# A list scheduler that keeps each PSUM bank to one engine at a time

## The chip, the cores and the metric

The kernel runs as one program on one core of a Trainium2 chip. The metric is the device time of one execution in microseconds (us). A core has five engines with in-order queues of their own: TensorE (PE), which multiplies matrices and writes its results into PSUM; VectorE (DVE) and ScalarE (ACT), which read PSUM and compute element by element; GpSimd (POOL), which here works on SBUF alone; and SyncE (SP), which issues the DMAs. PSUM has eight banks of 512 float32 numbers in each of 128 partitions. Engines wait for each other through semaphores.

## The reference

Two layers of a hybrid mixer work on 128 prompt tokens and 512 sample tokens, 640 in all, of width 1024, in float32. A layer normalises and modulates the input, projects it, sends the parts through three branches (latent attention, differential attention, a chunked mLSTM), gates each branch and projects back:

```python
h = rmsnorm(x, W['g_norm'][l]) * (1 + scale) + shift
proj = h @ W['W_in'][l]
...
o1 = attention(q_b[..., :DIFF_D], keys_b[..., :DIFF_D], vals_b, DIFF_SCALE)
o2 = attention(q_b[..., DIFF_D:], keys_b[..., DIFF_D:], vals_b, DIFF_SCALE)
o_b = rmsnorm(o1 - lam.astype(o1.dtype) * o2, W['diff_norm'][l]) * (1.0 - lam_init)
...
sw = jnp.einsum('bhtd,bhsd->bhts', qc, kc) * w_intra
...
y = jnp.concatenate([o_a.reshape(B, T, GROUP_W) * jax.nn.silu(z_a),
                     o_b.reshape(B, T, GROUP_W) * jax.nn.silu(z_b),
                     o_c.reshape(B, T, GROUP_W) * jax.nn.silu(z_c)], axis=-1) @ W['W_out'][l]
x_new = x + gate * y
```

## The kernel before

**Recording and planning.** The kernel's body does not issue instructions. Every call on an engine is recorded by `Plan.add`, and at the end `Plan.issue` links the operations by their data (`link`), plays them through a list scheduler (`simulate`) and issues them in the order of the start times that the scheduler gave. So every instruction of the profile has one line, L488, and places in the program have to be told by tile shapes and times. In `simulate` each engine takes, whenever it is free, the ready operation with the lowest number (program order) for which `may` finds its tiles' places vacant. An operation is ready when all operations that it depends on by data have ended by the costs of `cost` and the delays of `delay`.

**Data and banks.** `link` finds dependencies by the elements that operations touch. Only for PE does it keep a rule on whole banks (a matmul follows the last matmul in its bank). The program built from the order, on the other hand, gets its semaphore waits when it is issued, in the order of issue: two instructions of different engines on the same PSUM bank are put one behind the other there, also where they touch different elements or only read. Which of two such instructions goes first is therefore decided by the global order that the plan gives, not only by the order on each engine.

**Where engines share a bank.** Three helpers matter.

- `k_stack` (L1180): in the preparation of each of the four differential heads of a layer (`diff_prep`), PE transposes the head's keys into a two-bank tile `pkd`. ACT makes four rounded copies of 64 partitions by 640 columns (two maps, each copied to two halves of a stack) and four of 64 by 128; DVE subtracts each from the PSUM values for the low part. In the profile these are ACT `CAST slotsr<-banks` and DVE `TENSOR_TENSOR slotsr<-banks,slotsr`. The scores of that head use them some microseconds later.
- `attend` (L1193): probabilities are transposed into PSUM (PE `banks<-fix,slots 128x128`), copied by ACT to SBUF (`COPY slots<-banks`) and multiplied with the values on PE. For the prompt tokens (t = 4) this is one 128x128 transposition, one small ACT copy, one matmul.
- `pst` (L1102) in each mLSTM head: five 128x128 score matmuls of PE into one two-bank tile (`banks<-slots 128x128`), each then read by a DVE multiplication (`fix<-fix,banks 128x256`).

The weights come in 512 KB pieces through three raw buffers. ACT casts each piece to a high part (`CAST fixr<-fix`), and DVE or POOL computes the low part, which frees the raw buffer and lets SP issue the next load.

Of the kernel before, what the change touches and what calls it, by code (L numbers as in the profile page):

```python
# [121 lines left out]
class Plan:  # L122
# [87 lines left out]
    def free(ap):  # L210
# [2 lines left out]
            n *= s  # L213
        return n

    def cost(self, o):


        m, e, k = o["m"], o["eng"], o["k"]
        if m == "dma_start":  # L220
            out = o["outs"][0]
            return 430, 0, 4 * self.free(out) * int(out.shape[0]), False
        if e == "PE":
            if m == "transpose":
                return 109, 273, 0, False
            n = self.free(k["rhs"])
            if "float32r" in str(k["rhs"].dtype):
                return max(111, 0.4535 * n + 3), 175 + 0.4535 * n, 0, False
            return 2 * max(111, 0.845 * n), 280 + max(0, 0.845 * n * 2 - 110), 0, False
        if not o["outs"]:  # L230
            return 60, 60, 0, False
        n = max(self.free(x) for x in o["outs"] + o["ins"])
        ptr = any(self.is_ap(x) and self.free(x) == 1 and n > 2 for x in list(o["a"][1:]) + [k.get("scale"), k.get("bias")])
        psum = any("PSUM" in str(x.space) for x in o["ins"])
        if e == "ACT":
            t = 155 + 0.85 * n + (100 if ptr else 0) + (193 if "accum_out" in k else 0)
            if any("Ln" in str(x) for x in o["a"]):
                return t + 2500, t + 1300, 0, False
            return t - 95, t, 0, False
        two = m in ("tensor_tensor", "tensor_tensor_scan", "scalar_tensor_tensor")  # L240
        if e == "DVE":
            t = 145 + 1.06 * n
            if m == "tensor_copy" and not psum or m == "memset":
                t = 145 + 0.53 * n
            elif m == "tensor_tensor_scan":
                t = 145 + 2.08 * n
            elif ptr:
                t += 62
            return t - 80, t, 0, not psum and (two or m == "tensor_copy" or m == "tensor_scalar" and n > 1)
        if "pow" in str(k.get("op")):  # L250
            t = 400 + 155 * n
        elif m == "memset":
            t = 145 + 0.75 * n
        else:
            t = 165 + 2.2 * n
        return t - 40, t, 0, two
# [6 lines left out]
    def link(self):  # L263
        last, readers = {}, {}
        for i, o in enumerate(self.ops):
            pre, tiles = set(), set()
            for x in o["ins"]:
                n = x.tensor.name
                if n in self.tags:
                    tiles.add(n)  # L270
                if n.startswith("in_") or n.startswith("out_"):
                    continue
                for key, m in self.touch(x).items():
                    for w, wm in last.get(key, ()):
                        if wm & m:
                            pre.add(w)
                    readers.setdefault(key, []).append((i, m))
            for x in o["outs"]:
                n = x.tensor.name
                if n in self.tags:  # L280
                    tiles.add(n)
                if n.startswith("in_") or n.startswith("out_"):
                    continue
                for key, m in self.touch(x).items():
                    kept = []
                    for r, rm in readers.get(key, ()):
                        if rm & m:
                            if r != i:
                                pre.add(r)
                            rm &= ~m  # L290
                        if rm:
                            kept.append((r, rm))
                    if key in readers:
                        readers[key] = kept
                    kept = []
                    for w, wm in last.get(key, ()):
                        if wm & m:
                            if w != i:
                                pre.add(w)
                            wm &= ~m  # L300
                        if wm:
                            kept.append((w, wm))
                    kept.append((i, m))
                    last[key] = kept
            if o["eng"] == "PE":

                x = o["outs"][0]
                key = (x.tensor.name, int(x.offset) % int(x.tensor.shape[-1]) // 512)
                pre.update(last.get(key, ()))
                last[key] = [i]  # L310
            pre.discard(i)
            o["pre"], o["tiles"] = pre, tiles
            o["occ"], o["lat"], o["bytes"], o["port"] = self.cost(o)

    def simulate(self, prio, strict=None, place=None):
# [3 lines left out]
        n = len(ops)  # L319
        pre = [set(o["pre"]) for o in ops]  # L320
        if strict is not None:
            tail = {}
            for i in strict:
                e = ops[i]["eng"]
# [9 lines left out]
        vacant, bank = {i: -1.0 - i for i in range(43)}, place or {}  # L334
# [11 lines left out]
        have, queue = set(), {b: list(l) for b, l in self.tenants.items()} if place else {}  # L346
# [3 lines left out]
        ev, start, dma, port, cold = [], [0.0] * n, 0.0, 0.0, 0.0  # L350
# [3 lines left out]
        t = end = 0.0  # L354
        done = 0

        def may(o):
            for x in o["tiles"]:
                if x not in have:
                    tag = self.tags[x][0]  # L360
                    if place:
                        if not all(b in vacant and queue[b][0] == x for b in place[x]):
                            return False

                    elif live[tag] + rank[x] - nxt[tag] - sum(y < rank[x] for y in early[tag]) >= self.CAPS[tag]:
                        return False
                    elif not any(all(b in vacant for b in c) for c in self.PLACES[tag]):
                        return False
            return True
        while done < n:  # L370
            moved = True
            while moved:
                moved = False
                for e in ready:
# [4 lines left out]
                    while ready[e]:  # L379
                        it = heappop(ready[e])  # L380
                        o = ops[it[1]]
                        if may(o) and (not o["port"] or port <= t or strict is not None):
                            got = it
                            break
                        aside.append(it)
                        if len(aside) > 60:
                            break
# [5 lines left out]
                    o = ops[i]  # L393
# [31 lines left out]
                    if o["bytes"]:  # L425
                        dma = max(t + 2000, dma) + o["bytes"] / (390.0 if t > 6000 else 270.0)
                        fin = dma + 150
                    else:
                        fin = t + late + slow + o["lat"]
                    end = max(end, fin)  # L430
                    heappush(ev, (fin + 60, 1, i, ()))
                    heappush(ev, (free[e], 0, -1, ()))
                    for to, l in succ[i].items():
                        if to == e and (e == "PE" or strict is not None and not o["bytes"]):
# [14 lines left out]
            while True:  # L449
                t, kind, i, l = heappop(ev)  # L450
# [1288 lines left out]
```

## Time and profile before

| | before |
|---|---|
| median of 3 runs | 1355.46 us (1352.91 to 1355.83) |
| the profiled execution's own time | 1349.96 us |
| its span, first to last instruction | 1348.2 us |
| mean granted TensorE clock | 0.991 |
| busy: PE, PEld, DVE, ACT, POOL | 1293.0, 1208.7, 814.2, 631.4, 377.5 us |
| the chain that ended last: PE, DVE, ACT | 79%, 8%, 5% of the span |

Busy time of PE is counted from modelled ends of pipelined matmuls, so PE can be "busy" and still lose time. A line of the timeline view gives start and length of a run of like instructions, and in brackets the idle time of the engine before it with what ended it.

### The profile page before, as it was taken

The numbers are of one execution on the slowest core, as the hardware profiler recorded it, in microseconds if no ns is written. First come the engines' busy times: TensorE is split into PE (matmuls) and PEld (weight loads), VectorE is DVE, ScalarE is ACT, GpSimd is POOL, SyncE is SP. The second block draws the span as 40 slices with busy tenths as digits, with TensorE's granted clock in tenths as the row PEclk, the third lists the DMA queues.
The fourth block names the chain that finished last, engine by engine and source line by source line (L and its number), as shares of the span: only waits on it lengthen the run. The fifth ranks groups of instructions, "written<-read, shape, count | busy, mean of one in ns | idle before, by whom it ended". The sixth has DMA issues, their size and how long they took to land.

```text
span 1348.2 us, 24097 instructions
## 1 busy us (share of the span) xinstructions
PE 1293.0 (96%) x9300; PEld 1208.7 (90%) x9300; DVE 814.2 (60%) x1786; ACT 631.4 (47%) x1333; POOL 377.5 (28%) x335
## 2 busy tenths in 40 slices
PE   7999999999999999999989899999999999999995
PEld 3789999979899999899879899999799999989984
DVE  2576756675657356664465676575656545576446
ACT  4445535253455455245475345434343454524534
POOL 0413322243223014311433233333232212151132
PEclk9999999999999999999999999999999999999998
DMA  9533334364223214532741433434522211253163
GB/s 325 153 83 107 106 100 134 110 184 139 83 84 113 64 42 143 177 113 80 240 143 52 117 110 91 116 94 127 165 85 62 71 52 48 81 169 97 48 203 133
DMA packets 164643, 156.41 MB, mean 116 GB/s; under 512 B 14192, under 2 KB 130592, under 8 KB 164528
## 3 DMA queue, kind: packets, MB, share of 16 engines
q1 hardware_dynamic: 164528, 154.87, 37.9%
q8 instruction: 73, 1.20, 0.4%
q14 instruction: 42, 0.34, 0.1%
HBM read 131.38 MB, written 23.46 MB: 115 GB/s over the span
## 4 chain that ended last, share of the span: by engine, by line
PE 79%; DVE 8%; ACT 5%; issue 2%; DMA 1%; POOL 1%; DVEq 0%; SPq 0%; POOLq 0%; ACTq 0%
PE banks L488 79%; DVE slots L488 3%; DVE slotsr L488 2%; ACT slotsr L488 2%; DVE fixr L488 1%; ACT fixr L488 1%; DVE fix L488 1%; ACT slots L488 1%; POOL fixr L488 0%; POOL slots L488 0%; DMA xd<-slots 0%; DMA fix<-in_W_ukv 0%; DMA fix<-in_W_in 0%; DMA slots<-grow 0%; POOL fix L488 0%
## 5 line engine op out<-in xcount | busy, mean ns | idle before, releaser
L488 PE MATMUL banks<-fixr 128*128 128x256 f32 (+6 forms) x5732 | 818.3, 297 | 6.9 <-ACT fixr L488 3.2
L488 PEld LDWEIGHTS banks<-fixr 128*128 128x128 f32 (+1 forms) x5732 | 753.2, 184 | 23.7 <-ACT fixr L488 3.7
L488 PE MATMUL banks<-fixr,slotsr 128*128 128x512 f32 (+3 forms) x990 | 236.0, 375 | 0.5 <-ACT slotsr L488 0.3
L488 ACT ACTIVATE slots<-banks,fix 128x128 f32<-128x128 f32 (+3 forms) x250 | 144.0, 582 | 171.7 <-DVE fix L488 94.3
L488 ACT CAST fixr<-fix 128x1024 fp32r<-128x1024 f32 (+6 forms) x164 | 164.4, 1009 | 113.2 <-PE banks L488 73.1
L488 POOL TENSOR_TENSOR fixr<-fix,fixr 128x1024 fp32r<-128x1024 f32 (+4 forms) x51 | 121.3, 2379 | 338.4 <-ACT fixr L488 333.0
L488 PEld LDWEIGHTS banks<-fixr,slotsr 128*128 128x128 f32 x990 | 170.6, 189 | 26.2 <-ACT slotsr L488 0.8
L488 DVE TENSOR_TENSOR fixr<-fix,fixr 128x1024 fp32r<-128x1024 f32 (+5 forms) x114 | 146.1, 1286 | 61.4 <-ACT fixr L488 60.5
L488 ACT COPY slots<-banks 128x128 f32<-128x128 f32 (+3 forms) x212 | 85.9, 425 | 131.2 <-PE banks L488 126.8
L488 PE MATMUL banks<-fix,slots 128*128 128x128 f32 x808 | 121.3, 278 | 20.7 <-ACT slots L488 11.2
L488 POOL TENSOR_TENSOR slots<-slots,fix 128x128 f32<-128x128 f32 (+3 forms) x132 | 83.8, 650 | 197.0 <-DVE fix L488 90.0
L488 PEld LDWEIGHTS banks<-fix,slots 128*128 128x128 f32 x808 | 96.5, 144 | 32.2 <-ACT slots L488 13.8
L488 POOL TENSOR_TENSOR slots<-slots 128x512 f32<-128x512 f32 x70 | 86.6, 1240 | 137.7 <-DVE slots L488 104.1
L488 DVE TENSOR_REDUCE fix<-banks 128x1 f32<-128x640 f32 (+1 forms) x120 | 84.5, 712 | 63.7 <-PE banks L488 63.2
L488 PE MATMUL banks<-slots 128*128 128x128 f32 (+1 forms) x848 | 113.0, 277 | 4.1 <-DVE fix L488 3.1
L488 PEld LDWEIGHTS banks<-slots 128*128 128x128 f32 x848 | 104.0, 191 | 9.6 <-DVE fix L488 4.2
L488 DVE TENSOR_TENSOR slots<-banks,slots 128x512 f32<-128x512 f32 x80 | 54.8, 690 | 52.6 <-PE banks L488 49.4
L488 ACT ACTIVATE slots<-slots 128x640 f32<-128x640 f32 (+2 forms) x76 | 52.9, 696 | 61.3 <-DVE slots L488 46.6
L488 DVE TENSOR_TENSOR slotsr<-banks,slotsr 64x640 fp32r<-64x640 f32 (+1 forms) x88 | 55.3, 629 | 43.3 <-ACT slotsr L488 42.5
L488 DVE SCALAR_TENSOR_TENSOR slots<-slots,fix 128x511 f32<-128x511 f32 (+4 forms) x114 | 76.1, 684 | 4.6 <-ACT slots L488 1.8
L488 POOL TENSOR_TENSOR slotsr<-slots,slotsr 128x640 fp32r<-128x640 f32 x22 | 32.8, 1492 | 157.7 <-ACT slotsr L488 157.7
L488 PE MATMUL banks<-slots,fix 128*128 128x129 f32 (+1 forms) x384 | 62.9, 307 | 5.0 <-DVE fix L488 4.3
(72 smaller groups left out, 966.7 us busy)
## 6 DMA issues: line engine op xcount, KB each, us to landing
fix<-in_W_in SPq DMA_DIRECT2D x56, 512.0 KB
fix<-in_W_mod SPq DMA_DIRECT2D x35, 512.0 KB
xd<-slots SPq DMA_DIRECT2D x70, 256.0 KB
slots<-xd SPq DMA_DIRECT2D x70, 256.0 KB
fix<-in_W_in SPq DMA_DIRECT2D x64, 256.0 KB
fix<-in_W_out SPq DMA_DIRECT2D x24, 512.0 KB
slots<-grow SPq DMA_DIRECT2D x32, 256.0 KB
slots<-in_W_mod SPq DMA_DIRECT2D x26, 256.0 KB
```

Of the source, the lines that this page charges most:

```text
L488: o["f"](*[place(x) for x in o["a"]], **{k: place(x) for k, x in o["k"].items()})
```

## The change

Each operation gets the list of PSUM banks that it touches (`banks`, over the reach of its access pattern in the free dimension, without regard to partitions). While the scheduler plays the plan, `held` notes for each physical bank and engine when that engine's last operation there ends. `may` refuses an operation while another engine holds one of its banks; the engine then takes the next ready operation, and events at the ends wake it. Nothing else is changed: the operations, their costs and the rest of the rules are the same.

```diff
+    @staticmethod
+    def reach(ap):
+        return 1 + sum(abs(int(s)) * (int(n) - 1) for s, n in list(ap.ap)[1:])
...
             o["pre"], o["tiles"] = pre, tiles
+
+            o["banks"] = tuple({(x.tensor.name, int(x.offset) % int(x.tensor.shape[-1]) // 512 + j)
+                                for x in o["outs"] + o["ins"] if self.tags.get(x.tensor.name, "Q")[0] in ("pj", "sm", "S")
+                                for j in range(1 + (max(0, self.reach(x) - 1) + int(x.offset) % int(x.tensor.shape[-1]) % 512) // 512)})
...
+        held = [{} for _ in range(8)]
+
         def may(o):
+            for x, j in o["banks"]:
+                if x in have:
+                    for e, f in held[bank[x][j]].items():
+                        if e != o["eng"] and f + self.delay(e, o["eng"]) > t:
+                            return False
...
                     end = max(end, fin)
+                    for x, j in o["banks"]:
+                        held[bank[x][j]][e] = fin
                     heappush(ev, (fin + 60, 1, i, ()))
+                    if o["banks"]:
+                        for to in ("PE", "DVE", "ACT"):
+                            heappush(ev, (fin + self.delay(e, to), 0, -1, ()))
```

In the built program most rows stand where they stood: 8469 of the 8618 operations on PE keep their place in PE's queue, 1656 of 1786 on DVE, 1151 of 1178 on ACT, and all 331 on POOL. (The line of every instruction is L508 now instead of L488.) Three places, with the waits that the program has there:

On ACT, the key preparation of the third differential head of layer 0. The rows are the eight casts out of `pkd`, a weight cast, half of a gate, and the copy of the prompt tokens' transposed probabilities (`COPY`). Before:

```order
L488 CAST slotsr<-banks 64x640 [waits PE_49]
L488 CAST slotsr<-banks 64x640
L488 CAST slotsr<-banks 64x640 [waits DVE_49] x2
L488 CAST slotsr<-banks 64x128 [waits DVE_49]
L488 CAST slotsr<-banks 64x128 x3
L488 CAST fixr<-fix 128x1024 [waits DMAHW6_49,PE_49,Activation_49]
L488 ACTIVATE slots<-banks 128x320 [waits PE_49]
L488 COPY slots<-banks 128x128 [waits PE_49]
```

And now:

```order
L508 CAST slotsr<-banks 64x640 [waits PE_49]
L508 CAST slotsr<-banks 64x640 x3
L508 CAST slotsr<-banks 64x128 x4
L508 CAST fixr<-fix 128x1024 [waits DMAHW6_49,PE_49,Activation_49]
L508 ACTIVATE slots<-banks 128x320 [waits PE_49]
L508 COPY slots<-banks 128x128 [waits PE_49]
```

The order on ACT is the same; the three waits for DVE within the casts are gone. It is so at all eight heads. On DVE the eight subtractions now wait once for ACT instead of four times, and at the third head of layer 1 three reads of a finished projection tile (128x256 and 128x4x32), which stood behind the subtractions, stand ahead of them.

On PE, the score tile of the second mLSTM head of layer 0: `pst` (128x128), then the state updates (128x129) among projection matmuls (128x320). Before:

```order
L488 MATMUL banks<-slots 128x128 x2
L488 MATMUL banks<-slots 128x128 [waits DVE_49]
L488 MATMUL banks<-slots 128x128 x2
L488 MATMUL banks<-slots 128x129 x2
L488 MATMUL banks<-slots 128x129 [waits Activation_49]
L488 MATMUL banks<-fixr 128x320 [waits Activation_49]
L488 MATMUL banks<-fixr 128x320
L488 MATMUL banks<-slots 128x129 [waits DVE_49] x3
```

And now:

```order
L508 MATMUL banks<-slots 128x128 x5
L508 MATMUL banks<-slots 128x129 x2
L508 MATMUL banks<-slots 128x129 [waits Activation_49]
L508 MATMUL banks<-fixr 128x320 [waits Activation_49]
L508 MATMUL banks<-fixr 128x320 x2
L508 MATMUL banks<-slots 128x129 [waits DVE_49] x2
```

PE's wait for a DVE read in the middle of `pst` is gone, and one more projection matmul stands before the second half of the updates. It is so at six of the eight mLSTM heads; the other two had no such wait.

On ACT, before the first latent head of layer 0: casts of the query projection (128x320) and the key projection (128x384) out of PSUM, and the cast of a weight piece (`fixr<-fix 128x640`). Before:

```order
L488 CAST fixr<-banks 128x320 [waits DVE_49,PE_49] x2
L488 CAST fixr<-fix 128x640 [waits DMAHW6_49,DMAHW5_49,Activation_49]
L488 CAST fixr<-banks 128x384 [waits DVE_49,PE_49]
L488 CAST fixr<-fix 128x1024 [waits DMAHW3_49,PE_49,Activation_49]
L488 CAST fixr<-banks 128x384 [waits PE_49]
```

And now:

```order
L508 CAST fixr<-banks 128x320 [waits DVE_49,PE_49]
L508 CAST fixr<-fix 128x640 [waits DMAHW6_49,DMAHW5_49,Activation_49]
L508 CAST fixr<-banks 128x320 [waits DVE_49,PE_49]
L508 CAST fixr<-banks 128x384 [waits DVE_49,PE_49]
L508 CAST fixr<-fix 128x1024 [waits DMAHW3_49,PE_49,Activation_49]
```

The weight cast, which waits for its DMA, moved ahead of one cast out of PSUM. The same stands in layer 1, and four more weight casts moved ahead by a few rows elsewhere.

## Rows read from the trace of the kernel before

**Rows 1.** The page: span, and busy time of PE.

```profile
span 1348.2 us, 24097 instructions
PE 1293.0 (96%) x9300; PEld 1208.7 (90%) x9300; DVE 814.2 (60%) x1786; ACT 631.4 (47%) x1333; POOL 377.5 (28%) x335
```

**Rows 2.** Timeline of ACT, 407 to 416 us: start, length, instructions, [idle before <-releaser].

```profile
407.51 1.38 ACT L488 CAST slotsr<-banks 64x640 fp32r<-64x640 f32 x2 [0.22 <-PE banks L488]
409.78 0.69 ACT L488 CAST slotsr<-banks 64x640 fp32r<-64x640 f32 x1 [0.88 <-DVE slotsr L488]
...
412.94 1.08 ACT L488 CAST slotsr<-banks 64x128 fp32r<-64x128 f32 x4 [0.89 <-DVE slotsr L488]
414.04 1.04 ACT L488 CAST fixr<-fix 128x1024 fp32r<-128x1024 f32 x1
415.11 0.44 ACT L488 ACTIVATE slots<-banks 128x320 f32<-128x320 f32 x1
415.44 0.26 ACT L488 COPY slots<-banks 128x128 f32<-128x128 f32 x1
```

**Rows 3.** Timeline of DVE, the same stretch.

```profile
408.93 0.82 DVE L488 TENSOR_TENSOR slotsr<-banks,slotsr 64x640 fp32r<-64x640 f32 x1 [0.22 <-ACT slotsr L488]
...
414.04 2.04 DVE L488 TENSOR_TENSOR slotsr<-banks,slotsr 64x640 fp32r<-64x640 f32 x5 [1.14 <-ACT slotsr L488]
```

**Rows 4.** Timeline of PE at six prompt-token products (one row before the second).

```profile
356.05 0.49 PE L488 MATMUL banks<-fix,slots 128*128 128x128 f32 x2 [0.75 <-ACT slots L488]
...
413.68 0.27 PE L488 MATMUL banks<-fix,slots 128*128 128x128 f32 x1
415.75 0.49 PE L488 MATMUL banks<-fix,slots 128*128 128x128 f32 x2 [1.20 <-ACT slots L488]
...
475.05 0.49 PE L488 MATMUL banks<-fix,slots 128*128 128x128 f32 x2 [0.93 <-ACT slots L488]
...
1010.38 0.49 PE L488 MATMUL banks<-fix,slots 128*128 128x128 f32 x2 [1.18 <-ACT slots L488]
...
1070.42 0.46 PE L488 MATMUL banks<-fix,slots 128*128 128x128 f32 x2 [1.39 <-DVE fix L488]
...
1130.15 0.49 PE L488 MATMUL banks<-fix,slots 128*128 128x128 f32 x2 [1.66 <-ACT slots L488]
```

**Rows 5.** Timeline of DVE at 355 us, and of PE at 362 us.

```profile
355.61 3.43 DVE L488 TENSOR_TENSOR fixr<-fix,fixr 128x1024 fp32r<-128x1024 f32 x1
...
362.81 0.77 PE L488 MATMUL banks<-fix,slots 128*128 128x128 f32 x5 [1.41 <-DVE slots L488]
```

**Rows 6.** Timeline of PE in the mLSTM heads, first and last of six.

```profile
104.89 1.38 PE L488 MATMUL banks<-slots 128*128 128x128 f32 x10 [0.51 <-DVE fix L488]
...
850.60 1.61 PE L488 MATMUL banks<-slots 128*128 128x128 f32 x12 [0.51 <-DVE fix L488]
```

**Rows 7.** Timeline of PE at each layer's first differential head.

```profile
293.49 0.85 PE L488 MATMUL banks<-slotsr 128*128 128x320 f32 x4 [0.75 <-ACT slots L488]
...
297.99 0.33 PE L488 MATMUL banks<-fix,slots 128*128 128x128 f32 x1 [0.64 <-ACT slots L488]
...
947.34 0.82 PE L488 MATMUL banks<-slotsr 128*128 128x320 f32 x2 [1.93 <-DVE slotsr L488]
948.56 0.90 PE L488 MATMUL banks<-slotsr 128*128 128x320 f32 x2 [0.41 <-DVE slotsr L488]
```

**Rows 8.** Busy time by stretch: from:to, length, each engine (instructions), PEclk, DMA, GB/s.

```profile
948.50:951.00 2.50, 2.44 (x7) 2.10 (x8) 2.47 (x5) 0.00 (x0) 1.69 (x2) 0.53 0.00 0
...
1130.20:1135.00 4.80, 4.80 (x30) 4.80 (x30) 3.66 (x11) 1.38 (x3) 1.77 (x2) 0.66 0.47 160
```

**Rows 9.** Timeline of ACT before the first latent head of layer 0.

```profile
587.62 0.43 ACT L488 CAST fixr<-banks 128x320 fp32r<-128x320 f32 x1 [0.90 <-PE banks L488]
588.90 0.73 ACT L488 CAST fixr<-fix 128x640 fp32r<-128x640 f32 x1 [0.85 <-DMA fix<-in_W_ukv]
```

**Rows 10.** Who waited for whom: us in total, times, longest us.

```profile
ACT fixr L488 <- DMA fix<-in_W_uq: 3.0, 1, 3.0
```

## The prediction

> **What bounds the kernel now.** I read the busy times first: PE is at work for 1293.0 of 1348.2 us [rows 1], the other engines for far less, so a wait that goes elsewhere counts only where PE would have stood for it. Its ends are modelled, so the 96% is no proof; the weight loads' 90% [rows 1] say the same thing from another side.
>
> Then I read the timelines of ACT and DVE at one differential head [rows 2, 3]. The two engines take turns on the tile `pkd`: ACT stands 0.88 us for DVE, DVE 1.14 us for ACT, ACT 0.89 us again. No data asks for a cast to wait for a subtraction; it waits because both read the same bank and the issue order alternates. Next the timeline of PE, for its idle times that such turns lead to [rows 4 to 7], the stretches where PE's granted clock falls behind an idle [rows 8], and last ACT and the weight DMAs [rows 9, 10], since the change moves a few weight casts.
>
> The sum is made against the profiled execution's own time, 1349.96 us, which is its span of 1348.2 plus 1.8 around it. It lies 5.5 below the median of the runs shown, 1355.46; what I subtract from the one I subtract from the other.
>
> **The change part by part.** No instruction is added or removed: the work of every engine is the same, and the new rule costs nothing on the chip. What changes is who goes first on a bank, thus the waits.
>
> *Casts and subtractions of* `pkd`, *eight heads.* Now ACT makes its eight casts in a row: from 407.51, four of 0.69 (1.38 for two) and 1.08 for the four small ones [rows 2], so to 411.35, where before it ended at 412.94 + 1.08 = 414.02. ACT is free 2.7 us earlier. DVE waits once, to 411.35 + 0.22 = 411.6; its subtractions take 0.82 for a large one and (2.04 - 0.82)/4 = 0.31 for a small one [rows 3], together 4 x 0.82 + 4 x 0.31 = 4.5, so it ends at 416.1, as before (414.04 + 2.04). So the turns cost DVE nothing in the end, and the gain is ACT's.
>
> Here a rule of the Trainium skill speaks against the change (PSUM — Partial Sum Buffer, PSUM bank collisions raise a hardware error): two engines may work on one bank at once where they touch different quadrants of 32 partitions. The casts and the subtractions of the two 64-partition maps could by that run side by side, and holding the whole bank puts off DVE's first subtraction. The rows disagree for this program: the cast at 409.78 is of the other half than the subtraction of 408.93, and yet it waited 0.88 us for it [rows 2, 3]; the built program's waits go by whole banks. By the rule DVE's first subtraction would be put off from 408.93 to 411.6 for nothing, 2.7 us at each of eight heads; by the rows the sum loses nothing, since the last subtraction ends when it did.
>
> *Prompt tokens' products (A).* Six times PE stands before the product with the transposed probabilities of the prompt tokens, because the small ACT copy that it reads comes late: 0.75 + 1.20 + 0.93 + 1.18 + 1.39 + 1.66 = 7.1 us [rows 4]. At 415.75 the copy stood behind the casts on ACT. With these done at 411.35, the weight cast of 1.04 and the half gate of 0.44 [rows 2] end at 412.8; the transposition ends on PE at 413.68 + 0.27 = 413.95 [rows 4], and a copy of 0.26 is done near 414.3. PE has other matmuls until 415.75 - 1.20 = 414.55 [rows 4], so nothing is left of the idle, with 0.3 us to spare. At 1070.42 DVE ended the wait; its reads of a finished projection, behind the subtractions before, now stand ahead. At 1130.15 ACT's copy stood behind a read that waited for a DVE read of the same bank, and ACT now goes first there. Bounds: 3.5 (half stay, since the margin is thin) to 7.1. I take 7.1, the row of the worked case.
>
> *A chain through DVE (B).* PE stands 1.41 us at 362.81 for a DVE product, in a chain that comes from a subtraction of 3.43 us at 355.61 [rows 5]. No bank is in that subtraction, so only what stands behind it can move. Bounds 0 and 1.4; I take half, 0.7.
>
> *Score tile of the mLSTM heads (C).* In six heads PE waited 0.51 us in the middle of `pst` for a DVE read of that bank [rows 6], 6 x 0.51 = 3.1 us. All five matmuls now stand ahead of the reads. DVE starts its first read by four short matmuls later, and the state updates behind wait for DVE too, which can give a part back. Bounds 0 to 3.1; I take 2.4.
>
> *First differential head of a layer (D).* There no other work hides the preparation. PE stands 0.75 + 0.64 for ACT and 1.93 + 0.41 for DVE [rows 7]. ACT's are gone with its free 2.7 us: 1.4. DVE's subtractions end no earlier (above), so of its 2.34 I take a quarter, 0.6. Together 2.0; bounds 0 and 3.7.
>
> *The clock (E).* After the idles at 947.34 and 948.56 PE's granted clock is 0.53 for 2.5 us, after that at 1130.15 it is 0.66 for 4.8 us [rows 8]; 0.53 is close to the lower level of 1.2 of 2.4 GHz. Lost there: 0.47 x 2.5 + 0.34 x 4.8 = 2.8 us. The second goes with its idle (1.6), the first only if the whole idle goes; I take 1.6, bounds 0 and 2.8.
>
> *Weight casts that moved ahead (F).* Before the first latent head of each layer a cast of 0.73 us, which had waited for its DMA to 588.90, stands ahead of the cast out of PSUM that ran at 587.62 [rows 9]. That one now starts at 588.90 + 0.73 = 589.63, 2.0 us later. The rest of the query and key casts keep their time, and PE has the projection's tail to do meanwhile; if that cover is gone, it costs 2 x 2.0 = 4.0. Bounds 0 and -4.0; I take -0.8, a fifth, since only one of the casts is late.
>
> Sum: 7.1 + 0.7 + 2.4 + 2.0 + 1.6 - 0.8 = 13.0 us. That is 1349.96 - 13.0 = 1337.0 by the profiled execution and 1355.46 - 13.0 = **1342.5** by the median.
>
> **The rivals.** *Waits that come back one step later.* PE's idles go where they were read, but the next late thing takes their place: DVE's subtractions end when they did, so what hangs on them (the head's scores, the evacuations that stood behind them) is as late, and PE, early by then, waits there. For it: the equal end of 416.1, and the thin 0.3 us in A. Against it: in five of the six places of A ACT released PE [rows 4]. Then A gives its lower bound 3.5 and C and D half of what I took, 2.2: 5.7 together, 1349.8.
>
> *No change that can be measured.* Of PE's time, 4% is idle [rows 1], and the waits on banks lie on ACT and DVE, which have time to spare. If the gain of a head is taken up by the next wait on a weight or on POOL's low parts, or C and D give nothing and F takes its 4.0 from A's 3.5, the time stays near 1355.5. Against it: the idles of rows 4 are followed by work without a gap, so time won there should be kept. That the change does not do what it says falls under this case; the order speaks against it, as the waits are gone from the program.
>
> *Slower: ACT blocked by weight DMAs.* Six weight casts on ACT were put ahead of reads of PSUM. An in-order engine that meets a weight not yet landed holds all reads behind it, and with them the banks that PE wants to write. The longest such wait in the trace is 3.0 us [rows 10]; six of these give 18, less the 13.0 of the sum: 5 us slower, 1360.5. It decides from 13.0/6 = 2.2 us for each cast. Against it: two of the six do wait today, one of them 0.85 us [rows 9]; for the other four I see no sign that the weight is late.
>
> **How the numbers follow.** My forecast has 65 in 100, the waits one step later 18, no change 9, slower 8. The forecast's own range goes from all upper bounds, 7.1 + 1.4 + 3.1 + 3.7 + 2.8 = 18.1 or 1337.4, less the 2.6 by which the fastest run of before lies below its median, so 1334.8, to 1349. The range takes in the first rival and stops at the edge of no change: 1334 to 1355. A measurement of this kernel can tell about 0.2%, 2.7 us, from no change. Faster by more than that: the forecast and most of the first rival, 0.82; within it 0.10, slower 0.08.
>
> **What the profile after would show.** Right, if ACT's eight `pkd` casts run in one stretch of 3.9 us and DVE waits once for them; if the idles of PE before the products near 356, 415, 475, 1010, 1070 and 1130 are gone, not only moved; if no wait of 0.51 us is left in `pst`; and if the granted clock stays whole near 1132. F is seen as a wait of ACT for a weight near 590 and its like in layer 1, with PE idle behind it or not. The forecast is wrong if PE's idle time falls by less than half of 13 us, that is, if new waits on DVE stand behind the old places, or if ACT waits more for weight DMAs than it did.

## The result, and the profile after

| | before | after |
|---|---|---|
| median of 4 runs | 1354.75 us (1352.91 to 1355.83) | 1338.92 us (1337.19 to 1341.32) |
| ratio, 95% interval | | 0.9886 [0.9866, 0.9905] |
| the profiled execution's own time, span | 1349.96, 1348.2 us | 1339.23, 1337.5 us |

The change gained 15.8 us by the medians where 13.0 were forecast; 1338.92 lies 3.6 us below the forecast of 1342.5. By the two profiled executions it gained 10.7 us; why these differ is told with the experiments on the clock. The page's first rows, for [rows 1]:

```profile
span 1337.5 us, 24099 instructions
PE 1290.5 (96%) x9300; PEld 1208.5 (90%) x9300; DVE 811.5 (61%) x1786; ACT 630.6 (47%) x1333; POOL 376.9 (28%) x335
```

Adding up PE's idle times of over 0.15 us one by one gives 37.0 us in 44 places before, and 28.8 in 36 after. The timeline of ACT at the third head of layer 0, for [rows 2]:

```profile
407.76 3.86 ACT L508 CAST slotsr<-banks 64x640 fp32r<-64x640 f32 x8
411.65 1.05 ACT L508 CAST fixr<-fix 128x1024 fp32r<-128x1024 f32 x1
412.72 0.44 ACT L508 ACTIVATE slots<-banks 128x320 f32<-128x320 f32 x1
413.06 0.26 ACT L508 COPY slots<-banks 128x128 f32<-128x128 f32 x1
```

And of DVE, for [rows 3]:

```profile
411.66 4.54 DVE L508 TENSOR_TENSOR slotsr<-banks,slotsr 64x640 fp32r<-64x640 f32 x8 [2.48 <-ACT slotsr L508]
```

The eight casts run in one stretch and end at 411.62 (411.35 was worked out), DVE waits once and ends at 416.20 (416.1), and the copy of the prompt tokens is done at 413.3. ACT's waits for these subtractions, 21.4 us in 23 places before, no longer occur in the list of waits. PE at the six products, for [rows 4], and at the places where it now stands instead:

```profile
354.92 0.49 PE L508 MATMUL banks<-fix,slots 128*128 128x128 f32 x2
...
413.37 0.49 PE L508 MATMUL banks<-fix,slots 128*128 128x128 f32 x2
...
416.77 3.11 PE L508 MATMUL banks<-fixr 128*128 128x256 f32 x24 [0.66 <-DVE slots L508]
421.06 0.77 PE L508 MATMUL banks<-fix,slots 128*128 128x128 f32 x5 [1.03 <-DVE slots L508]
...
473.79 0.40 PE L508 MATMUL banks<-fix,slots 128*128 128x128 f32 x2
...
1002.72 0.41 PE L508 MATMUL banks<-fix,slots 128*128 128x128 f32 x2
...
1009.68 0.77 PE L508 MATMUL banks<-fix,slots 128*128 128x128 f32 x5 [1.16 <-DVE slots L508]
...
1062.24 0.47 PE L508 MATMUL banks<-fix,slots 128*128 128x128 f32 x2
...
1120.12 0.41 PE L508 MATMUL banks<-fix,slots 128*128 128x128 f32 x2
...
1125.77 0.77 PE L508 MATMUL banks<-fix,slots 128*128 128x128 f32 x5 [0.24 <-DVE slots L508]
```

All six idles are gone. At three of the six heads PE stands some microseconds later, for DVE: 0.66 and 1.03 us at one, 1.16 us at another, 0.24 us at the last. The other terms, for [rows 5 to 7]: what stands behind the score tile of the first mLSTM head, the score tile of the second (16 matmuls in one run), the chain through DVE (at 361.69), and the first differential head of each layer.

```profile
109.05 0.57 PE L508 MATMUL banks<-fixr 128*128 128x320 f32 x2 [0.55 <-DVE slots L508]
...
149.61 1.95 PE L508 MATMUL banks<-slots 128*128 128x128 f32 x16
151.35 0.71 PE L508 MATMUL banks<-fixr 128*128 128x320 f32 x3
...
286.16 0.71 PE L508 MATMUL banks<-slotsr 128*128 128x320 f32 x3 [0.37 <-DVE slotsr L508]
...
297.80 0.77 PE L508 MATMUL banks<-fix,slots 128*128 128x128 f32 x5 [0.58 <-ACT slots L508]
...
361.69 0.77 PE L508 MATMUL banks<-fix,slots 128*128 128x128 f32 x5 [1.43 <-DVE slots L508]
...
941.54 0.71 PE L508 MATMUL banks<-slotsr 128*128 128x320 f32 x3 [0.61 <-DVE slotsr L508]
942.09 1.79 PE L508 MATMUL banks<-fixr,slotsr 128*128 128x512 f32 x7
943.71 0.46 PE L508 MATMUL banks<-slotsr 128*128 128x320 f32 x2
944.48 0.56 PE L508 MATMUL banks<-slotsr 128*128 128x320 f32 x2 [0.30 <-DVE slotsr L508]
```

No wait of 0.51 us is left in a score tile. At the first mLSTM head, though, PE stands 0.55 us for DVE right behind the tile, so there the idle has only moved.

Last the weight cast before the first latent head of layer 0, on ACT, for [rows 9], and what PE does then:

```profile
587.16 0.73 ACT L508 CAST fixr<-fix 128x640 fp32r<-128x640 f32 x1 [2.23 <-DMA fix<-in_W_ukv]
587.79 0.80 ACT L508 CAST fixr<-banks 128x320 fp32r<-128x320 f32 x2
```

```profile
588.64 0.41 PE L508 MATMUL banks<-fixr 128*128 128x320 f32 x1 [0.74 <-ACT fixr L508]
588.90 0.31 PE L508 MATMUL banks<-slotsr,fixr 128*128 128x320 f32 x1
589.66 0.56 PE L508 MATMUL banks<-fixr 128*128 128x320 f32 x2 [0.46 <-DVE fixr L508]
```

ACT waits 2.23 us for the weight, and two casts out of PSUM wait behind it. PE stands 0.74 + 0.46 us, where before it stood 0.37 for ACT; in layer 1 0.29 + 0.46 us at 1219 and 1220, where before it did not stand. PE before, and ACT's waits for the two weights that it waits longer for now (in us in total, times, longest; before 1.2 us and 1.3 us in total):

```profile
590.05 0.41 PE L488 MATMUL banks<-fixr 128*128 128x320 f32 x1 [0.37 <-ACT fixr L488]
```

```profile
ACT fixr L508 <- DMA fix<-in_W_ukv: 4.0, 2, 2.2
ACT fixr L508 <- DMA fix<-in_W_mod: 3.7, 6, 1.8
```

### The profile page after: what moved, and what is told of

Read it like the earlier page. It is cut to its first block, busy times and chain, and to the rows that moved or that the text cites. A ratio compares the mean times of both kernels' runs of the same rounds, so it can differ in the third digit from the quotient of the medians.

```text
span 1337.5 us, 24099 instructions
## 1 busy us (share of the span) xinstructions
PE 1290.5 (96%) x9300; PEld 1208.5 (90%) x9300; DVE 811.5 (61%) x1786; ACT 630.6 (47%) x1333; POOL 376.9 (28%) x335
## 4 chain that ended last, share of the span: by engine, by line
PE 80%; DVE 8%; ACT 4%; issue 2%; DMA 1%; POOL 1%; DVEq 0%; POOLq 0%; ACTq 0%; SPq 0%
PE banks L508 80%; DVE slots L508 3%; DVE slotsr L508 2%; ACT slotsr L508 2%; DVE fixr L508 2%; DVE fix L508 1%; ACT slots L508 1%; DMA fix<-in_W_mod 1%; ACT fixr L508 1%; POOL fix L508 0%; POOL slots L508 0%; ACT fix L508 0%; DMA xd<-slots 0%; DMA fix<-in_W_ukv 0%; POOL fixr L508 0%
## 5 line engine op out<-in xcount | busy, mean ns | idle before, releaser
L508 PE MATMUL banks<-fixr 128*128 128x256 f32 (+6 forms) x5732 | 820.2, 297 | 9.2 <-ACT fixr L508 3.8
L508 PEld LDWEIGHTS banks<-fixr 128*128 128x128 f32 (+1 forms) x5732 | 754.2, 185 | 26.3 <-ACT fixr L508 4.5
L508 PE MATMUL banks<-fixr,slotsr 128*128 128x512 f32 (+3 forms) x990 | 235.0, 375 | 0.0
L508 ACT ACTIVATE slots<-banks,fix 128x128 f32<-128x128 f32 (+3 forms) x250 | 144.0, 583 | 174.2 <-DVE fix L508 98.7
L508 ACT CAST fixr<-fix 128x1024 fp32r<-128x1024 f32 (+6 forms) x164 | 164.4, 1009 | 116.5 <-PE banks L508 72.1
L508 POOL TENSOR_TENSOR fixr<-fix,fixr 128x1024 fp32r<-128x1024 f32 (+4 forms) x51 | 122.3, 2399 | 320.9 <-ACT fixr L508 320.7
L508 PEld LDWEIGHTS banks<-fixr,slotsr 128*128 128x128 f32 x990 | 169.9, 189 | 24.7
L508 DVE TENSOR_TENSOR fixr<-fix,fixr 128x1024 fp32r<-128x1024 f32 (+5 forms) x114 | 145.1, 1276 | 65.3 <-ACT fixr L508 58.2
L508 ACT COPY slots<-banks 128x128 f32<-128x128 f32 (+3 forms) x212 | 85.4, 425 | 131.4 <-PE banks L508 115.6
L508 POOL TENSOR_TENSOR slots<-slots,fix 128x128 f32<-128x128 f32 (+3 forms) x132 | 82.8, 643 | 201.9 <-DVE fix L508 88.4
L508 PE MATMUL banks<-fix,slots 128*128 128x128 f32 x808 | 121.7, 279 | 15.7 <-DVE slots L508 9.7
L508 POOL TENSOR_TENSOR slots<-slots 128x512 f32<-128x512 f32 x70 | 86.3, 1235 | 139.7 <-DVE slots L508 102.7
L508 DVE TENSOR_REDUCE fix<-banks 128x1 f32<-128x640 f32 (+1 forms) x120 | 84.7, 713 | 65.5 <-PE banks L508 65.1
L508 PEld LDWEIGHTS banks<-fix,slots 128*128 128x128 f32 x808 | 96.8, 144 | 26.8 <-DVE slots L508 8.4
L508 PE MATMUL banks<-slots 128*128 128x128 f32 (+1 forms) x848 | 111.6, 277 | 1.0 <-ACT slots L508 1.0
L508 PEld LDWEIGHTS banks<-slots 128*128 128x128 f32 x848 | 103.7, 191 | 5.1 <-ACT slots L508 2.9
L508 DVE TENSOR_TENSOR slots<-banks,slots 128x512 f32<-128x512 f32 x80 | 55.1, 691 | 52.8 <-PE banks L508 50.6
L508 ACT ACTIVATE slots<-slots 128x640 f32<-128x640 f32 (+2 forms) x76 | 52.9, 696 | 60.8 <-DVE slots L508 45.6
L508 DVE SCALAR_TENSOR_TENSOR slots<-slots,fix 128x511 f32<-128x511 f32 (+4 forms) x114 | 76.5, 686 | 4.5 <-ACT slots L508 1.7
L508 POOL TENSOR_TENSOR slotsr<-slots,slotsr 128x640 fp32r<-128x640 f32 x22 | 32.1, 1460 | 157.6 <-ACT slotsr L508 157.6
L508 DVE TENSOR_TENSOR slotsr<-banks,slotsr 64x640 fp32r<-64x640 f32 (+1 forms) x88 | 55.3, 629 | 34.1 <-ACT slotsr L508 33.0
L508 PE MATMUL banks<-slots,fix 128*128 128x129 f32 (+1 forms) x384 | 63.2, 308 | 5.0 <-DVE fix L508 4.5
```

Source lines behind the costliest of these rows:

```text
L508: o["f"](*[place(x) for x in o["a"]], **{k: place(x) for k, x in o["k"].items()})
```

## The experiments

All ratios are to the kernel before, run beside on the same chip.

**The rule for one tile, for all others, and the order of issue alone.** The main question was whether the gain comes from the waits themselves or from the plan laid out anew. Two kernels limit the rule by the tile's name:

```diff
-  if self.tags.get(x.tensor.name, "Q")[0] in ("pj", "sm", "S")
+  if self.tags.get(...)[0] in ("pj", "sm", "S") and x.tensor.name.startswith("pkd")       # pkd_only
+  if self.tags.get(...)[0] in ("pj", "sm", "S") and not x.tensor.name.startswith("pkd")   # all_but_pkd
```

Three more leave the kernel before and its order on every engine as they are, and move only the order of issue across engines:

```diff
-  for i in sorted(range(len(self.ops)), key=lambda i: (start[i], i)):
+  order = sorted(range(len(self.ops)), key=lambda i: (start[i], i))
+  for i in self.casts_first(order):     # order_pkd: ACT's operations up to the last cast of a pkd, before its first subtraction
+  for i in self.scores_first(order):    # order_pst: PE's operations up to the fifth score matmul, before the first read
+  for i in self.scores_first(self.casts_first(order)):    # order_both
```

> The rule on banks holds for the tile of the differential keys alone. Theory (waits on banks by the order of issue): the six idles of PE before the prompt-token products and those of the first heads go, the 0.51 us waits in the score tile of the mLSTM heads stay; 8 us faster than before, about 1347. Rival (the gain comes from the whole plan being laid out anew, with 757 tiles on other banks): no simple share, anything from 1339 to 1355, and the six idles stay or go without regard to this tile.

> The rule on banks holds for every tile but that of the differential keys. Theory: the 0.51 us waits go, worth 4.7 us by the gaps that closed in the trace after, the weight casts before the latent heads cost 1.5, and the six idles before the prompt-token products stay: 3 to 5 us faster than before, about 1351, and with the kernel that has the rule for that tile alone the two gains add up to that of the full change. Rival: the gains do not add up, since each place is limited by the next.

> The kernel before, with its plan and the order on every engine untouched; only in the order of issue across engines do the eight casts of a differential head's keys come ahead of the subtractions. Theory: this alone takes the waits away, so it gains what the rule for that tile alone gains, 6 to 8 us, about 1347. Rival (new plan, not the waits): within 2 us of the kernel before, 1354.

> The kernel before, with its plan and every engine's order untouched; only in the order of issue across engines do the five score matmuls of an mLSTM head come ahead of the reads of their bank. Theory: six idles of 0.51 us go, and with the restart of the weight loads behind each some 0.8, so 4.5 us faster, about 1350. Rival (an idle costs its length): 3.1 us or less, as forecast 2.4, about 1352.

> The kernel before, every engine's order untouched; the order of issue across engines is changed at both places, the differential keys and the score tiles. Theory: the waits that the order of issue alone takes away are worth 4.1 + 4.7 = 8.8 us, about 1345.6, and what is left to the full change (5 to 6 us) is that the engines take other work meanwhile. Rival (the two gains overlap as those of the rule by tile do, 11.5 + 10.3 against 14.6): 5 to 6 us, about 1349.

| | median us | ratio, interval |
|---|---|---|
| the change once more (control) | 1339.83 | 0.9892 [0.9874, 0.9910] |
| pkd_only | 1342.92 | 0.9917 [0.9901, 0.9933] |
| all_but_pkd | 1344.08 | 0.9926 [0.9911, 0.9940] |
| order_pkd | 1350.29 | 0.9966 [0.9952, 0.9980] |
| order_pst | 1349.75 | 0.9967 [0.9954, 0.9980] |
| order_both | 1346.19 | 0.9935 [0.9920, 0.9950] |

The order of issue alone is worth 4.1 us, 4.7, and 8.8 together (1355.0 - 1346.19), as expected of the two in sum. So waits that come from the order of issue are shown as a cause, with no engine's order changed. They are a little over half of the 14.6 us that the control gained. The other 5.8 us go with the new plan, in which engines take other work meanwhile and tiles stand on other banks; no run separates these two. Single expectations missed: pkd_only gained 11.5 us and not 8, all_but_pkd 10.3 and not 3 to 5, and order_pkd 4.1 and not 6 to 8, so for the tile of the keys the order of issue is a good third of what the rule gains. PE in order_pkd, at the fifth and sixth of the six products:

```profile
1070.65 0.46 PE L503 MATMUL banks<-fix,slots 128*128 128x128 f32 x2 [0.98 <-DVE fix L503]
...
1129.96 0.49 PE L503 MATMUL banks<-fix,slots 128*128 128x128 f32 x2 [1.26 <-ACT slots L503]
```

The idles near 356, 415, 475 and 1010 are gone there, too, though PE stands for DVE a little later at two of these heads (0.74 us near 421, 0.72 + 0.34 us near 1013 and 1017). Of the last two idles 0.98 and 1.26 us stay. For the fifth the timeline of DVE says why, in order_pkd at 1065 us and in the change at 1056:

```profile
1065.13 4.54 DVE L503 TENSOR_TENSOR slotsr<-banks,slotsr 64x640 fp32r<-64x640 f32 x8 [2.25 <-ACT slotsr L503]
1069.68 0.42 DVE L503 TENSOR_TENSOR slots<-banks,fix 128x256 f32<-128x256 f32 x1
```

```profile
1056.03 0.42 DVE L508 TENSOR_TENSOR slots<-banks,fix 128x256 f32<-128x256 f32 x1 [0.42 <-PE banks L508]
1056.38 0.48 DVE L508 TENSOR_TENSOR fix<-banks,fix 128x128 f32<-128x128 f32 x2
1057.86 4.54 DVE L508 TENSOR_TENSOR slotsr<-banks,slotsr 64x640 fp32r<-64x640 f32 x8 [1.00 <-ACT slotsr L508]
```

With the casts ahead and nothing else moved, DVE stands 2.25 us with the reads of a projection tile behind it in its queue, and PE waits for these reads. In the change they fill a part of DVE's wait, which is left at 1.00 us. The first differential head of layer 1 shows the same on PE. In order_pkd it stands almost as long as the 1.93 + 0.41 us of [rows 7], in three parts:

```profile
945.84 0.71 PE L503 MATMUL banks<-slotsr 128*128 128x320 f32 x3 [0.61 <-DVE slotsr L503]
947.63 0.53 PE L503 MATMUL banks<-slotsr 128*128 128x320 f32 x2 [1.08 <-DVE slotsr L503]
948.77 0.86 PE L503 MATMUL banks<-slotsr 128*128 128x320 f32 x2 [0.60 <-DVE slotsr L503]
```

In the change seven projection matmuls stand at the second of these places (942.09 above), and 0.61 + 0.30 us are left.

The two parts of the rule gained 11.5 and 10.3 us, 7.2 more than the control. Two overlaps are seen, where each rule takes away something before the same product. The idle of 1.66 us before the sixth is gone in pkd_only and down to 0.38 us in all_but_pkd; the matmuls behind it stand 3.1 and 2.5 us earlier, the fall of the clock that [rows 8] show there included. The idle of 0.75 us before the first is gone in both, worth 0.9 and 0.7 us; the other four stay in all_but_pkd. What the rest of the 7.2 is stays open; the intervals of the three ratios make it uncertain by some 4 us.

In order_pst the six idles are gone, too. How much earlier the matmuls behind a place start, counted against those ahead of it and against the profile before, says what an idle was worth: 0.27 us at the first place, then 0.58, 0.43, 0.51, 0.58 and 0.45, together 2.8. So an idle of 0.51 us cost no more than about its own length by the trace, and the theory of a restart behind it falls. (The median's 4.7 us, 2.7 to 6.2 by the interval, is not told apart from these 2.8.) In the control the six places gave 0 (the idle of 0.55 us above comes in), 0.75, 0.98, 1.10, 0.74 and 0.99, together 4.5. There a third projection matmul stands between scores and updates, as in the rows of 151.35 above, while DVE finishes its reads.

**The rule by quadrants.** Each bank's entry is kept four times, by 32 partitions:

```diff
-  held = [{} for _ in range(8)]
+  held = [[{} for _ in range(4)] for _ in range(8)]
...
-  for x, j in o["banks"]:
+  for x, j, q in o["banks"]:      # q: each quarter of the partitions that the operation touches
...
-      for e, f in held[bank[x][j]].items():
+      for e, f in held[bank[x][j]][q].items():
```

> The changed kernel, with the rule on banks kept by quadrants of 32 partitions, so that the plan lets ACT cast one 64-partition map of the keys while DVE subtracts the other. The program's waits are still made for whole banks. Theory (the program's waits decide): the plan takes turns again on that tile, ACT's 0.9 us waits for DVE are back, and the time is that of the kernel without the rule for that tile, about 1344. Rival (finer rule, more overlap): no slower than the full change, 1339 or less.

Measured 1343.98 us, 0.9927 [0.9914, 0.9939], as expected. The list of waits (total, times, longest), for before's 21.4 us in 23 places, and ACT at the head of [rows 2]:

```profile
ACT slotsr L509 <- DVE slotsr L509: 19.0, 22, 1.3
```

```profile
410.71 0.69 ACT L509 CAST slotsr<-banks 64x640 fp32r<-64x640 f32 x1 [0.88 <-DVE slotsr L509]
412.28 0.54 ACT L509 CAST slotsr<-banks 64x128 fp32r<-64x128 f32 x2 [0.89 <-DVE slotsr L509]
```

A finer rule than the one by which the program gets its waits brings the turns back. The Trainium skill (PSUM — Partial Sum Buffer, PSUM bank collisions raise a hardware error) says that accesses in different quadrants of a bank may overlap. No run here lets them, so whether this kernel could gain by it was not tried. With the program's waits as they are, the planner's rule must not be finer.

**The clock.** The control is the change unaltered, before_again the kernel before unaltered.

> The changed kernel once more, as the measure for the others of this series. Chance theory of the clock: the dip of TensorE's granted clock between 94 and 100 us (0.51 where the kernel before had 1.00 after the same two idles) is an accident of that one execution, and a second profile of the same program shows 1.00 there, with the span near 1335. Rival: the new order of instructions causes it, and it is there again. Time: 1339, 15 us under the kernel before.

> The kernel before once more. Its one profiled execution (1349.96 us) ran below all timed ones (median 1354.4), and in it the granted clock fell to 0.5 four times before the tail, 3.4 or 6.8 us long each. Theory (clock): in a usual execution it falls at more of the idles that the change takes away (near 415, 1010, 1070), so this profile shows five or more such falls, a span near 1352, with the idles themselves as before. Rival: the same falls, and the extra time is spread over the whole span.

before_again took 1354.05 us with a span of 1352.2. Windows of the change, of the control and of before_again behind the two idles near 92 us (the granted clock stands third from the end), and one of before_again behind the idle at its sixth product:

```profile
92.00:100.00 8.00, 6.79 (x35) 6.58 (x34) 4.20 (x11) 2.22 (x8) 1.60 (x2) 0.57 0.74 210
```

```profile
92.00:100.00 8.00, 6.79 (x56) 6.37 (x55) 4.92 (x13) 3.62 (x10) 1.15 (x2) 1.00 0.74 213
```

```profile
92.50:101.00 8.50, 7.29 (x39) 7.08 (x39) 4.16 (x11) 2.23 (x8) 1.66 (x2) 0.60 0.72 201
1135.00:1140.00 5.00, 4.36 (x39) 4.36 (x40) 4.27 (x11) 1.97 (x6) 2.37 (x2) 1.00 0.37 112
```

One program has the fall at 92 us in one execution and not in another: 35 matmul records against 56 in the same 8 us. So it is chance, and no effect of the change. My reason for before's faster profile was wrong as to place: before_again has the five falls and the span that were expected, but none near 415, 1010 or 1070. Its falls near 22, 92 and 755 are longer or further ones, behind idles that every kernel here has. Ahead of the tail the clock was down for 27.3 us in all, against 17.1 in the profile of [rows 1 to 10], and most of the 4 us between that profile and the timed runs is that. The fall at 1131 of [rows 8] is chance as well: behind the same idle of 1.67 us the clock is 1.00 here. Near 948 both profiles of the kernel before show a fall and neither of the change's does, but all_but_pkd, where PE stands 1.93 + 0.68 us at this place, has none either.

**What the change left.** Two weight casts go back behind the next cast out of PSUM (casts_behind); on top of this, two low parts of weights and three reads of a tile go behind the sums of a head's norm on DVE (norm_first); then DVE's low part of the same two weights goes back as well (both_behind).

```diff
   order = sorted(range(len(self.ops)), key=lambda i: (start[i], i))
+  for w in (5890, 11923):                                   # casts_behind: the casts of W_ukv
+      k = order.index(w)
+      to = next(j for j in range(k + 1, len(order)) if self.ops[order[j]]["eng"] == "ACT")
+      order.insert(to, order.pop(k))
+  for group, after in (((3432, 3674), 3257), ((9788, 10053), 9446),      # norm_first: low parts, with the load that each lets go
+                       ((3819, 3820, 3821), 3857), ((3822,), 3858)):     # and the reads of a projection tile
+      order = [i for i in order if i not in group]
+      k = order.index(after) + 1
+      order[k:k] = group
...
```

> The changed kernel with two weight casts put back behind the next cast out of PSUM, one before each layer's first latent head. Theory: the two idles near 584 and 585, and near 1217 and 1218, 0.9 us a layer, go: 1.5 us faster than the full change, about 1338 (ratio to before 0.988). Rival (PE waits there for the weight itself, whoever goes first): no change from the full change.

> The kernel with two weight casts put back behind a cast out of PSUM once more, beside the other two on the same chip: 1337 to 1338.5, 1.5 us under the full change, if the first measurement holds; 1339 if it was chance.

> The changed kernel with the two weight casts put back, and three moves on DVE: the low part of a weight piece, twice, and three reads of a projection tile, once, stand behind the sums of a head's norm instead of ahead of them. Theory (what the change left late is DVE's order, not a bank): the idles of PE for DVE near 361 (1.4 us), 417 (0.8) and 1009 (1.2) go, 2 to 3 us faster than with the weight casts alone, about 1335. Rival (the norm's chain is late for another reason, or the weight piece is missed later): the idles stay or come back elsewhere, 1337.

> The kernel with the norm's sums first, and now DVE's low part of the same two weight pieces, too, stands behind the subtraction out of PSUM, as in the kernel before (with the casts alone put back, PE's idle near 586 and 1218 only changed its releaser from ACT to DVE, 0.8 us). Theory: PE goes without the 0.8 us twice, and the cost of the moved weight casts is undone only when both engines are put back: 1.5 us under the kernel with the norm's sums first, about 1335. Rival: PE waits there for the weight whoever goes first; 1336.5.

| | median us | ratio, interval |
|---|---|---|
| casts_behind | 1337.44 | 0.9878 [0.9864, 0.9892] |
| casts_behind2, the same again | 1338.34 | 0.9881 [0.9865, 0.9898] |
| norm_first | 1336.47 | 0.9866 [0.9849, 0.9883] |
| both_behind | 1334.69 | 0.9866 [0.9849, 0.9882] |

PE before the first latent head in casts_behind, then in both_behind:

```profile
585.54 0.42 PE L513 MATMUL banks<-fixr 128*128 128x320 f32 x1 [0.44 <-ACT fixr L513]
...
586.88 0.56 PE L513 MATMUL banks<-fixr 128*128 128x320 f32 x2 [0.78 <-DVE fixr L513]
```

```profile
584.59 0.41 PE L528 MATMUL banks<-fixr 128*128 128x320 f32 x1 [0.26 <-ACT fixr L528]
...
585.54 0.56 PE L528 MATMUL banks<-fixr 128*128 128x320 f32 x2 [0.39 <-DVE fixr L528]
```

With the casts alone put back PE stands as long as after the change (1.22 us against 1.20), now mostly for DVE, whose low part had moved too; with both it stands 0.65. The second measurement of the same kernel lies in the range expected of it, but neither interval is clear of the change's, and the gain by the medians is not at this place. PE in norm_first:

```profile
359.84 0.76 PE L520 MATMUL banks<-fix,slots 128*128 128x128 f32 x5 [0.72 <-DVE slots L520]
...
417.22 0.77 PE L520 MATMUL banks<-fix,slots 128*128 128x128 f32 x5
```

The idle of 1.43 us is halved and those at 416.8 and 421 are gone; that at 1009 only fell to 0.98. So these idles hang, at least in part, on DVE's order behind the subtractions. both_behind has the lowest median, but it was timed beside a lower median of the kernel before (1353.83 us against 1355.0), and its ratio is that of norm_first. So it is not shown to be faster than norm_first, and the intervals of both still overlap the change's.

## Why the prediction was right, point by point

**Casts and subtractions:** right in mechanism and in size, to 0.3 us on ACT and 0.1 on DVE. The order of issue as cause is shown by order_pkd and order_both.

**A, 7.1 taken:** the six idles went, but I closed the books at the place itself. With 0.66 + 1.03, 1.16 and 0.24 us given back to DVE, 7.1 - 3.1 = 4.0 are left (the control gives back 0.80, 1.20 and 0.24, so 4.9 are left). That is the first rival's mechanism, at three heads of six: DVE's subtractions end when they did, PE is there earlier. The step that failed is "nothing is left of the idle" as a whole account.

**B, 0.7 taken:** nothing, 1.41 before and 1.43 after. A subtraction of a weight's low part and evacuations stand before the norm's sums on DVE, and the rule doesn't touch those; norm_first moved them.

**C, 2.4 taken, 3.1 as bound:** too small, bound included. The six places gave 4.5 in the control, all of it at five of them; at the first the wait only came back one step later. The order alone gives 2.8, near what I read in [rows 6]. The projection matmul moved into the next wait, which the order shown ahead of the prediction has, goes with the rest, and I had counted that wait as a loss.

**D, 2.0 taken:** 3.73 - 0.37 - 0.58 - 0.61 - 0.30 = 1.9, but with the parts exchanged. Of ACT's 0.75 + 0.64 a wait of 0.37 for DVE and 0.58 for ACT are left; DVE's 1.93 + 0.41 fell to 0.91, although its subtractions end no earlier. Seven projection matmuls (128x512) now stand between the scores, where PE waited before: again the work taken meanwhile, which I had left out, and which the order of issue alone does not bring (2.29 us are left there in order_pkd).

**E, 1.6 taken:** the granted clock was 1.00 at both places after, but that the fall at 1131 would go with its idle was no effect of the change: before_again keeps the idle and has no fall. The size was luck. Over all timed executions on record the mean granted clock is 0.9865 for the kernel before (44 of them) and 0.9889 for the change and its control (8). At some 1350 us that is at most 3.2 us, an estimate from these two means that takes PE to be at work throughout; where in the kernel it lies is open.

**F, -0.8 taken:** right in mechanism, too small. PE stands 0.74 + 0.46 - 0.37 = 0.8 us longer in layer 0 and 0.75 in layer 1: -1.6. I followed only the cast on ACT; DVE's low part of the same weight had moved as well. With both put back (both_behind) 0.65 us are left in layer 0, 0.28 more than before, and what these are is open.

The terms measured sum to about 4.0 + 0 + 4.5 + 1.9 - 1.6 = 8.8 us by the traces without the clock, close to the 8.2 us by which PE's idle time fell. With at most 3.2 of the clock that makes 12.0, and the median's 15.8 (12.9 to 18.2 by the interval) leaves some 4 us open. The profiles' own differences, 10.7 and 12.8 (1348.2 - 1335.4), are against the fast execution of [rows 1]. The forecast came out near the median partly by luck: A was too large where C was too small; and the basis, one execution with few falls of the clock, hid about 4 us that a usual one of the kernel before takes.

Of the signs of being wrong that the prediction names, two were seen in part: new waits on DVE stand behind some of the old places, and ACT waits more for weights. Neither was large enough, as PE's idle time fell by 8.2 us, more than half of 13. The rival of blocked casts did not decide: ACT's waits for W_ukv grew from 1.2 to 4.0 us in all and those for W_mod from 1.3 to 3.7, together 5.2 us, where it needed 13, and PE, by term F, stood for 1.6 us more.

## What to carry to other kernels

Where waits are made from the order of issue, a planner has to know the rule by which they are made. Here a finer rule gave back about 4 us (1343.98 against 1339.83); a coarser one was not tried. The waits alone were a little over half of the gain; the rest came with the new plan, and the traces show part of it as work that an engine takes while it would have stood. When an idle closes, follow the same engine for the next ten microseconds before counting it, and follow every engine's part of a moved step, not only the one that is seen to wait. Take a second profile of an unaltered kernel before a difference of a few microseconds is explained.

## What the hardware showed that I had not expected

In the profiles' clock records each fall of the clock is 3.4 or 6.8 us long at half speed, but for the one at the end of the program. Behind the same idles of 1.7 and 1.2 us near 92 us the clock fell in the change and in before_again, and stayed whole in the control. The same subtraction of 128x1024 took 1.2 us on DVE in 78 of 94 places in the kernel before, and 1.4 to 3.4 us in most of the others: 3.4 near 355 us, 2.7 near 166. Near 355 us it took 2.8 us in the change and 1.2 in norm_first, which moved it.
